# One layer of a hybrid attention trunk: attention's small products gathered into fewer bursts between the large products

## The chip, the cores and the metric

The kernel runs on one NeuronCore of a Trainium2 chip. The metric is the device time of one execution in microseconds (us); lower is better. TensorE (PE) does the matrix products, VectorE (DVE) and ScalarE (ACT) the elementwise work, SyncE (SP) issues the loads.

## The reference

One layer of a causal decoder trunk on 256 tokens of width 1024, in float32. One input projection of the normed input feeds two attentions side by side: eight heads of softmax attention (called MoBA in the code; the whole sequence is one block, so it is plain causal attention) and four heads of gated linear attention (GLA). Their outputs go through one output projection, and a gated feed-forward part of width 2816 follows.

```python
xn = rms_norm(x, attn_norm_g[l])
proj = xn @ w_in[l]
mq = rope(split_heads(proj[..., o_mq:o_mk], MOBA_HEADS), pos)
mk = rope(split_heads(proj[..., o_mk:o_mv], MOBA_HEADS), pos)
mv = split_heads(proj[..., o_mv:o_gq], MOBA_HEADS)
y_moba = merge_heads(moba_attention(mq, mk, mv))
...
og = gla_attention(gq, gk, gv, split_heads(log_a, GLA_HEADS))
...
x = x + jnp.concatenate([y_moba, y_gla], axis=-1) @ w_out[l]
hn = rms_norm(x, ffn_norm_g[l])
h = causal_dwconv(hn @ w_ffn_up[l], conv_w[l], conv_b[l])
h_gate, h_val = h[..., :D_FF], h[..., D_FF:]
x = x + (jax.nn.silu(h_gate) * h_val) @ w_ffn_down[l]
return rms_norm(x, final_norm_g)
```

## The kernel before, in words

The projections are the **large products**. Each float32 weight is split into a high and a low part (`split_hi`, line 92, ScalarE; `split_lo`, line 95, VectorE), and three products (`mm3`, lines 109 to 111) make one float32-exact sum. The input projection runs over q = 0 to 47: six groups of columns (G, q, k, v, gv, r) times eight contraction tiles. The output projection runs over q = 48 to 63, and behind it the feed-forward part runs over 22 pairs of column tiles to the end.

Attention is laid between the large products. A table `plan` says at which q a piece of attention is emitted: `on(q, f, ...)` appends it, and `emit(q)` calls what stands at q, in the order of the `on` calls, ahead of the large products of that q. On TensorE the instructions stand in just that order. On VectorE and ScalarE a scheduler of the language orders what was emitted.

The pieces that matter here are these.

- GLA's score matrix is built in seven levels (`LEVELS`, numbered 0 to 6 here). `lvl_a` and `lvl_b` (lines 329 to 331, 344, 350) make a level's factors on VectorE and ScalarE, in two pairs of tiles kt and qt that the levels use in turn. `lvl_c` is the level's product on TensorE (line 362; line 357 for level 6). `lvl_d_` is the level's copy out of its bank: a predicated copy on VectorE (line 376), or for level 6 a copy on ScalarE (line 371).
- Softmax attention goes by pairs of heads. `m_scores` (line 486) makes the scores of a pair in two banks. `m_softmax1` (lines 494, 496, 499) and `m_softmax2` (lines 505 to 507) make the probabilities of a head. `m_pt` transposes them, three transposes a head (line 514), with a copy on ScalarE (line 516). `m_av` is the value product of a pair (lines 526, 527), with its copies at lines 530 and 531.
- `l128_c` (line 401) and `g_av` (lines 418 to 421) are GLA's last products.

All these small products write to tiles that `att()` hands out from the pool `ps_att`: four PSUM banks, used in turn. A new tile waits until the last reader of its bank's tile before it is done. The transposes have a tile each, so has a level, a head's scores and a pair's value product.

The three transposes of a head are called pt0 to pt7 below, the value products av0 to av3, the level products c0 to c6, the scores s0 to s3. A **burst** is what stands on TensorE between two large products. The 16 bursts from q = 25 on are, before: c0; c1; c2 s0; c3 s1; pt0; pt1; c4 s2; pt2; c5 av0 pt3; s3; pt4; c6 av1 pt5; pt6; l128_c av2 pt7; g_av; av3.

Of the kernel before, what the change touches and what calls it, by code (L numbers as in the profile page):

```python
# [9 lines left out]
F32 = mybir.dt.float32  # L10
# [6 lines left out]
S = 256  # L17
KT = 8
HM, HD = 8, 64
# [6 lines left out]
EPS = 1e-6  # L26
NG = 256 + RANK + 256
LEVELS = [32, 16, 8, 4, 2, 1, 64]
# columns of the parameter array
P_FG, P_BG, P_CW, P_CB = 0, 8, 10, 10 + 3 * 2 * NP  # L30
# [4 lines left out]
def trunk_kernel(ctx: ExitStack, tc: tile.TileContext, xT_d, wG_d, w5_d, wo_d, up_d, dn_d,  # L35
# [16 lines left out]

    # ------------------------------------------------------------------ constants and parameters
    A.preload_act_table_set("natural_log_exp_and_others")
# [12 lines left out]

    # the tensor engine's clock rises while the first loads are under way
    warm = const.tile([128, 128], F32, name="warm")
# [4 lines left out]

    # ------------------------------------------------------------------ weights: load and split
    RAW, SPL = 4, 3
# [59 lines left out]

    # ------------------------------------------------------------------ x
    xg = main.tile([128, KT + KT * S], F32, name="xg")     # the first norm's gains, then x^T
    pag = xg[:, :KT]
# [33 lines left out]
    def rsqrt_t(r, ss, n, tmp):  # L173
        """r = (ss / n + EPS) ** -0.5 by logarithm and exponential, then a Newton step."""
        v, t = tmp
        V.tensor_scalar(v, ss, 1.0 / n, EPS, op0=ALU.mult, op1=ALU.add)
        A.activation(t, ss, AF.Ln, scale=1.0 / n, bias=eps)
        A.activation(r, t, AF.Exp, scale=-0.5)
        V.tensor_mul(t, r, r)
        V.scalar_tensor_tensor(t, t, -0.5, v, op0=ALU.mult, op1=ALU.mult)  # L180
        V.scalar_tensor_tensor(r, t, 1.5, r, op0=ALU.add, op1=ALU.mult)

    def rsqrt(r, ss, n, tmp):
        """r = (ss / n + EPS) ** -0.5: a seed from the exponent bits, then Newton steps. It yields
        between its steps, so that other work fits in."""
        v, t = tmp
        V.tensor_scalar(v, ss, 1.0 / n, EPS, op0=ALU.mult, op1=ALU.add)
        V.tensor_scalar(t.bitcast(I32), v.bitcast(I32), 1, None, op0=ALU.logical_shift_right)
        yield
        V.tensor_scalar(r.bitcast(I32), t.bitcast(I32), -1.0, float(0x5F3759DF),  # L190
                        op0=ALU.mult, op1=ALU.add)
        for _ in range(3):
            V.tensor_mul(t, r, r)
            yield
            V.scalar_tensor_tensor(t, t, -0.5, v, op0=ALU.mult, op1=ALU.mult)
            V.scalar_tensor_tensor(r, t, 1.5, r, op0=ALU.add, op1=ALU.mult)

    # ------------------------------------------------------------------ attention buffers
    ap_ = ctx.enter_context(ExitStack())
# [4 lines left out]
    Gc = at.tile([128, 512], F32, name="Gc")  # L204
    ATd = at.tile([128, 8, 64], F32, name="ATd")           # the blocks of 64 on the diagonal
    ATu = at.tile([128, 8, 64], F32, name="ATu")           # the second half's columns
    AT01 = at.tile([128, 4, 128], F32, name="AT01")
# [43 lines left out]
    def xrow():  # L251
        """The rotation's tables take up the norm, which lies along their rows here."""
        p = att()
        for tt in range(2):
            T.matmul(p[:, tt * 128:(tt + 1) * 128], rstd(tt).to_broadcast([128, 128]), ident,
                     start=True, stop=True)
        for t in (cos, sin):
            V.tensor_mul(t, t, p[:, :S])

    # ---- GLA  # L260
    def g_evac(tt):
# [19 lines left out]
    def g_diag():  # L281
        dgp = at.tile([128, 2, 256], F32, name="e", bufs=2)
        V.scalar_tensor_tensor(dgp, gqk[:, :, 0:256], DK ** -0.5, gqk[:, :, 272:528],
                               op0=ALU.mult, op1=ALU.mult)
        V.tensor_add(id64, ident[:, 0:64], ident[:, 64:128])
        dg = at.tile([128, 2, 2, 2], F32, name="dg")       # pair, ttile, head
        for tt in range(2):
            V.tensor_reduce(dg[:, :, tt, :], dgp[:, tt].rearrange("p (a h d) -> p a h d", a=2, h=2),
                            axis=mybir.AxisListType.X, op=ALU.add)
        for i in range(8):  # L290
            A.activation(ATd[:, i], id64, AF.Copy, scale=dg.rearrange("p a b c -> p (a b c)")[:, i:i + 1])
# [147 lines left out]
    def g_tail():  # L439
        # the norm's tables before the gate's: one change of tables  # L440
        with tc.manual_schedule(engines={mybir.EngineType.Activation}):
            for tt in range(2):
                g_norm(tt)
            for tt in range(2):
                gr_evac(tt)
# [12 lines left out]

    # ---- MoBA (the sequence is one block, so a query's own block is all it attends to)
    def rope_a(which, n):  # L460
        """The halves of each head change places."""
        qs = at.tile([128, 512], F32, name="qs", bufs=2)
        for i in range(4):
            a, b = 32 * i, 32 * (i ^ 1)
            A.activation(qs[a:a + 32], st["qk"[which]][n][b:b + 32], AF.Copy)  # L465
        st["rope", which, n] = qs.rearrange("p (a t) -> p a t", a=2)
# [12 lines left out]
    def m_scores(pr):  # L479
        # two heads in turn, each in its half of the array's rows and in a bank of its own  # L480
        for hh in range(2):
            st["s", 2 * pr + hh] = att()
        for c0, c1 in ((0, 128), (128, 384)):
            for hh in range(2):
                ps = slice(64 * hh, 64 * hh + 64)
                T.matmul(st["s", 2 * pr + hh][:, c0:c1], mqT[ps, pr, c0:c0 + 128], mkT[ps, pr, 0:c1 - c0],
                         start=True, stop=True)
# [44 lines left out]

    # ------------------------------------------------------------------ emission plan
    plan = {}

    def on(q, f, *a):
        plan.setdefault(q, []).append((f, a))
# [25 lines left out]
    for l in range(7):  # L563
        b = 21 + 11 * l // 4
        on(b, lvl_a, l)
        on(b + 1, lvl_b, l)
        on(b + 4, lvl_c, l)
        on(b + 5, lvl_d_, l)
    on(b + 5, lvl_join)
# [3 lines left out]
    for tt in range(2):  # L573
# [3 lines left out]
        on(40, gv_evac, tt)  # L577
    for h in range(HM):
        b = 30 + 3 * h // 2
        if h % 2 == 0:  # L580
            on(b, m_scores, h // 2)
        on(b + 1, m_softmax1, h)
        on(b + 2, m_softmax2, h)
        on(b + 4, m_pt, h)
        if h % 2:
            on(b + 7, m_av, h // 2)
    on(46, g_av, 0)
# [24 lines left out]
    for q in range(48):  # L612
        g, k = divmod(q, 8)
# [28 lines left out]

    # ------------------------------------------------------------------ output projection
    hh_ = main.tile([128, KT, S], F32R, name="hh", tag="ah")
# [33 lines left out]

    # ------------------------------------------------------------------ feed-forward
    downs = {}  # L680
# [91 lines left out]

    # the output's columns by bank; the last ones, which end the kernel, are fewer
    PIECES = (((0, 512), (512, 1024)), ((0, 512), (512, 768), (768, 1024)))
# [10 lines left out]
    def residual(tt, n):  # L785
        """The residual opens the down projection's sums."""
        a, b = PIECES[tt][n]
# [22 lines left out]

    # pair 0: its last contraction tile waits for the last columns of h
    up_alloc(0)
# [11 lines left out]
    lo(2, 1)  # L824
    # pair 1
    dload(1)
# [7 lines left out]
    for n, _ in enumerate(steps):  # L834
        if n < 4:
            ups[3].split_lo(512 * n, 512 * n + 512)
    # pair 2
    dload(2)
# [17 lines left out]
    gate_lo(0)  # L856
    # pair 3
    dload(3)
# [63 lines left out]
    A.preload_act_table_set("sqrt_and_others")  # L922
    # the last pair's gate is awaited behind one product of the second token tile
    for i in range(NP - 4, NP - 1):
# [10 lines left out]

    # ------------------------------------------------------------------ final norm
    fin = ff.tile([128, 24], F32, name="fin")
    yy = ff.tile([128, 2, D], F32, name="yy", tag="big")
    for tt in range(2):
# [4 lines left out]
        for n, (a, b) in enumerate(PIECES[tt]):  # L944
# [11 lines left out]
            if n < last:  # L956
                vb = v
                V.tensor_scalar(vh, v, -0.5, None, op0=ALU.mult)
        # r = (mean square + EPS) ** -0.5 with one Newton step
        A.activation(sq, ss, AF.Sqrt, scale=1.0 / D, bias=vb)  # L960
# [10 lines left out]
def _layout(inputs):  # L971
# [5 lines left out]
    def ktile(m):  # L977
        return m.reshape(-1, 128, m.shape[1]).transpose(1, 0, 2)      # [128, k, cols]

# [14 lines left out]
    fin_g = f(np.broadcast_to(a["final_norm_g"].reshape(1, D), (128, D)))  # L994
    # tables that depend on shapes alone
    inv = (1.0 / (np.float32(10000.0) ** (np.arange(0, HD, 2, dtype=np.float32) / np.float32(HD)))).astype(np.float32)
# [32 lines left out]
```

## Time and profile before

| | us |
|---|---|
| median of 3 runs (321.97 to 322.44) | 322.04 |
| span of the profiled execution, first to last instruction | 320.4 |
| what lies around the span (the difference of the two) | 1.6 |
| PE busy in the span | 312.3 |
| DVE busy in the span | 253.7 |
| ACT busy in the span | 203.2 |

The page gives the profiled execution by its span. With the 1.6 us around it, it stands for the median, 322.04 us. A busy PE is not a PE at its peak: matmuls are pipelined, so the distance from one start to the next tells what a product costs, and the duration of one does not. The rows in use are in the section after next.

### The profile page before, as it was taken

To read this page: it belongs to the slowest core of one execution; us is meant where nothing else is said; L and a number is where in the kernel's file an instruction comes from. 1 tells how busy PE (TensorE), PEld (TensorE's weight loads), DVE (VectorE), ACT (ScalarE), POOL (GpSimd) and SP (SyncE) were. 2 spreads that over 40 slices of the span, in tenths; PEclk is the share of its full clock that TensorE was granted. 3 is DMA by queue.
4 is the path that set the end of the run, shared out by engine and by line. 5 is a ranking of instruction groups with operands and counts; after the bars stand their busy time and mean duration, and the time that the engine had idled before them with its cause. 6 is when DMAs were issued, how large, how long until landed. Compare 5 with 4: busy or idle time off the path is not lost.

```text
span 320.4 us, 5873 instructions
## 1 busy us (share of the span) xinstructions
PE 312.3 (97%) x2312; PEld 285.9 (89%) x2312; DVE 253.7 (79%) x478; ACT 203.2 (63%) x369; POOL 3.5 (1%) x16
## 2 busy tenths in 40 slices
PE   8999999999999999999999999999999999999992
PEld 7999997776766999999999999999999999999982
DVE  3888999999634658899999987777787777776653
ACT  5978988588845748637677655555555555544353
POOL 4000000000000000000000000000000000000000
PEclk9999999999999999999999999999999999999997
DMA  6999433452360245379356555555555521110003
GB/s 186 387 415 402 183 133 131 139 186 79 125 262 1 103 163 190 140 282 370 127 212 254 202 196 196 199 196 198 197 196 199 218 111 68 65 67 1 2 0 132
DMA packets 12299, 55.39 MB, mean 173 GB/s; under 512 B 1376, under 2 KB 2928, under 8 KB 7920
## 3 DMA queue, kind: packets, MB, share of 16 engines
q1 hardware_dynamic: 12272, 55.02, 46.2%
q8 instruction: 18, 0.29, 0.4%
q14 instruction: 9, 0.07, 0.1%
HBM read 53.97 MB, written 1.05 MB: 172 GB/s over the span
## 4 chain that ended last, share of the span: by engine, by line
PE 79%; DVE 9%; ACT 5%; issue 2%; DMA 2%; SPq 1%; DVEq 0%; ACTq 0%
PE att L110 14%; PE att L109 14%; PE att L111 14%; PE acc L110 10%; PE acc L109 10%; PE acc L111 10%; DVE lo L95 2%; DMA xg<-in_xT 2%; ACT qs L465 1%; DVE qt L350 1%; DVE att L494 1%; PE att L421 1%; PE att L420 1%; PE att L526 1%; DVE ATd L376 1%
## 5 line engine op out<-in xcount | busy, mean ns | idle before, releaser
L92 ACT ACTIVATE hi<-raw 128x1024 fp32r<-128x1024 f32 (+3 forms) x84 | 80.1, 971 | 51.4 <-PE att L110 43.1
L95 DVE TENSOR_TENSOR lo<-raw,hi 128x1024 fp32r<-128x1024 f32 (+3 forms) x86 | 93.7, 1098 | 13.8 <-ACT hi L92 13.8
L109 PE MATMUL att<-hh,hi 128*128 128x256 f32 x352 | 98.6, 280 | 0.0
L111 PE MATMUL att<-hh,lo 128*128 128x256 f32 x352 | 98.4, 280 | 0.0
L110 PE MATMUL att<-hl,hi 128*128 128x256 f32 x352 | 98.4, 279 | 0.0
L109 PEld LDWEIGHTS att<-hh,hi 128*128 128x128 f32 x352 | 66.3, 188 | 0.0
L111 PEld LDWEIGHTS att<-hh,lo 128*128 128x128 f32 x352 | 66.2, 188 | 0.0
L110 PEld LDWEIGHTS att<-hl,hi 128*128 128x128 f32 x352 | 66.2, 188 | 0.0
L756 DVE SCALAR_TENSOR_TENSOR c<-us,par,c 128x256 f32<-128x256 f32 x88 | 40.7, 482 | 4.1 <-ACT c L748 2.5
L748 ACT ACTIVATE c<-us,par 128x256 f32<-128x256 f32 x44 | 24.0, 590 | 21.6 <-DVE us L738 16.1
L111 PE MATMUL acc<-dhi,gl 128*128 128x512 f32 (+1 forms) x88 | 32.3, 367 | 0.0
L110 PE MATMUL acc<-dlo,gh 128*128 128x512 f32 (+1 forms) x88 | 32.2, 366 | 0.0
L109 PE MATMUL acc<-dhi,gh 128*128 128x512 f32 (+1 forms) x88 | 31.8, 361 | 0.0
L695 DVE TENSOR_TENSOR dlo<-draw,dhi 128x1024 fp32r<-128x1024 f32 x22 | 26.7, 1220 | 0.0
L738 DVE TENSOR_TENSOR us<-att,rb 128x512 f32<-128x512 f32 x20 | 13.8, 690 | 15.9 <-PE att L111 15.9
L109 PE MATMUL acc<-hi,ah 128*128 128x512 f32 (+1 forms) x64 | 25.9, 404 | 0.2 <-ACT hi L92 0.2
L110 PE MATMUL acc<-lo,ah 128*128 128x512 f32 (+1 forms) x64 | 24.6, 384 | 0.4 <-DVE lo L95 0.4
L111 PE MATMUL acc<-hi,al 128*128 128x512 f32 (+1 forms) x64 | 24.1, 376 | 0.0
L690 ACT ACTIVATE dhi<-draw 128x1024 fp32r<-128x1024 f32 x22 | 23.1, 1048 | 0.0
L110 PEld LDWEIGHTS acc<-dlo,gh 128*128 128x128 f32 x88 | 16.5, 188 | 3.0
L109 PEld LDWEIGHTS acc<-dhi,gh 128*128 128x128 f32 x88 | 16.6, 188 | 2.9
L111 PEld LDWEIGHTS acc<-dhi,gl 128*128 128x128 f32 x88 | 16.5, 188 | 2.6
(192 smaller groups left out, 537.5 us busy)
## 6 DMA issues: line engine op xcount, KB each, us to landing
raw<-in_up SPq DMA_DIRECT2D x22, 1024.0 KB, 4.8
draw<-in_dn SPq DMA_DIRECT2D x22, 512.0 KB, 5.7
raw<-in_w SPq DMA_DIRECT2D x8, 1024.0 KB, 7.4
raw<-in_wo SPq DMA_DIRECT2D x4, 1024.0 KB, 4.7
raw<-in_w SPq DMA_DIRECT2D x4, 512.0 KB, 7.6
raw<-in_wG SPq DMA_DIRECT2D x2, 528.0 KB, 7.2
out_y<-yy SPq DMA_DIRECT2D x4, 256.0 KB, 2.2
raw<-in_wG SPq DMA_DIRECT2D x3, 264.0 KB, 4.8
```

The source lines that it names most:

```text
L92: A.activation(self.hi[:, a:b], self.raw[:, a:b], AF.Copy)
L95: V.tensor_sub(self.lo[:, a:b], self.raw[:, a:b], self.hi[:, a:b])
L109: T.matmul(out, sh, mh, start=first, stop=False, **kw)
L110: T.matmul(out, sh, ml, start=False, stop=False, **kw)
L111: T.matmul(out, sl, mh, start=False, stop=last, **kw)
L350: V.tensor_mul(o, q_, e_)
L376: V.copy_predicated(o, m, p[:, :256].rearrange("p (i n b) -> p i n b", i=8, b=b))
L690: A.activation(hi, downs[i][0], AF.Copy)
L695: V.tensor_sub(lo, d, hi)
L738: V.tensor_tensor(u[:, :, 2:], upo[i][2].rearrange("p (a t) -> p a t", a=2), rb[:, None, :].to_broadcast([128, 2, S]), op=ALU.mult)
L748: A.activation(cv[i][:, a], u[:, a, 2:], AF.Identity, bias=par[:, P_CB + m:P_CB + m + 1], scale=par[:, P_CW + 2 * 2 * NP + m:P_CW + 2 * 2 ...
L756: V.scalar_tensor_tensor(c[:, a], u[:, a, w:w + S], par[:, wc:wc + 1], c[:, a], op0=ALU.mult, op1=ALU.add)
```

## The change

Three places of the plan change. Level 0's product moves from q = 25 to q = 27 and its copy from 26 to 28, so c0 and c1 stand in one burst. The transposes of the two heads of a pair are emitted together, at q = 35, 38, 41 and 44, behind the value product of the pair before, which stands at the same q. The last value product, av3, moves from q = 47 to q = 46, ahead of `g_av`. The ten bursts are then: c0 c1; c2 s0; c3 s1; pt0 pt1; c4 s2; c5 av0 pt2 pt3; s3; c6 av1 pt4 pt5; l128_c av2 pt6 pt7; av3 g_av. No instruction is added or removed.

```diff
     for l in range(7):
         b = 21 + 11 * l // 4
         on(b, lvl_a, l)
         on(b + 1, lvl_b, l)
-        on(b + 4, lvl_c, l)
-        on(b + 5, lvl_d_, l)
+        on(b + 4 if l else 27, lvl_c, l)
+        on(b + 5 if l else 28, lvl_d_, l)
...
-    for h in range(HM):
-        b = 30 + 3 * h // 2
-        if h % 2 == 0:
-            on(b, m_scores, h // 2)
-        on(b + 1, m_softmax1, h)
-        on(b + 2, m_softmax2, h)
-        on(b + 4, m_pt, h)
-        if h % 2:
-            on(b + 7, m_av, h // 2)
+    for pr in range(HM // 2):
+        b = 30 + 3 * pr
+        on(b, m_scores, pr)
+        for hh in range(2):
+            on(b + 1 + hh, m_softmax1, 2 * pr + hh)
+            on(b + 2 + hh, m_softmax2, 2 * pr + hh)
+        on(min(b + 8, 46), m_av, pr)
+        on(b + 5, m_pt, 2 * pr)
+        on(b + 5, m_pt, 2 * pr + 1)
```

The rest of the diff drops comments. Lines from 640 on stand two further down.

The first place is TensorE at q = 38, before (c5, av0, pt3). Numbers are those of buffers: att_960 is c5's bank tile, att_972 that of av0, att_979 that of pt3; the name in brackets is the engine whose count the instruction waits for.

```order
L362 MATMUL att_960<-qt1_131,kt1_129 64x64 [waits DVE_49]
L362 MATMUL att_960<-qt1_131,kt1_129 64x64 x7
L526 MATMUL att_972<-pt_863,mv_143 64x256 [waits Activation_49]
L527 MATMUL att_972<-pt_863,mv_143 64x128
L526 MATMUL att_972<-pt_885,mv_143 64x256
L527 MATMUL att_972<-pt_885,mv_143 64x128
L514 MATMUL att_979<-ident_78,pe_894 128x128 [waits Activation_49]
L514 MATMUL att_979<-ident_78,pe_894 128x128 x2
```

The same place now (c5 is att_954, av0 att_966, pt2 att_973, pt3 att_979):

```order
L362 MATMUL att_954<-qt1_131,kt1_129 64x64 [waits DVE_49,Activation_49]
L362 MATMUL att_954<-qt1_131,kt1_129 64x64 x7
L526 MATMUL att_966<-pt_879,mv_143 64x256 [waits DVE_49,PE_49]
L527 MATMUL att_966<-pt_879,mv_143 64x128
L526 MATMUL att_966<-pt_885,mv_143 64x256
L527 MATMUL att_966<-pt_885,mv_143 64x128
L514 MATMUL att_973<-ident_78,pe_863 128x128 [waits Activation_49]
L514 MATMUL att_973<-ident_78,pe_863 128x128 x2
L514 MATMUL att_979<-ident_78,pe_894 128x128 [waits DVE_49]
L514 MATMUL att_979<-ident_78,pe_894 128x128 x2
```

pt2 has come into this burst, six large products later than it was, and pt3 now waits for VectorE where it waited for ScalarE. In the built program pt3's tile lies in the bank that c5 used in the same burst, so the count it waits for is that of c5's copy (line 376). Before, its bank was that of pt2, which ScalarE had copied out.

The second place is VectorE where it makes c5's copy, before (c5 is att_960; kt0 and qt0 are level 6's factors, d_1002 belongs to `l128_a`, pe_947 to head 4):

```order
L95 TENSOR_TENSOR lo_951<-raw_664,hi_950 128x1024 [waits DMAHW0_49,Activation_49]
L505 RECIPROCAL mx_943<-mx_943 128x2 [waits Activation_49]
L385 TENSOR_TENSOR d_1002<-Gc_123 128x256
L507 TENSOR_SCALAR pe_947<-pe_947,mx_943 128x256 [waits DVE_49]
L376 COPY_PREDICATED ATd_124<-lvl_77,att_960 128x256 [waits PE_49]
L344 TENSOR_TENSOR kt0_128<-gkT_122,e_933 128x4x64 [waits Activation_49]
L350 TENSOR_TENSOR qt0_130<-gqT_121,e_933 64x4x64 x2
L531 TENSOR_TENSOR ml_98<-att_972,mh_326 128x256 [waits Activation_49]
```

And now (c5 is att_954):

```order
L95 TENSOR_TENSOR lo_945<-raw_664,hi_944 128x1024 [waits DMAHW0_49,Activation_49]
L344 TENSOR_TENSOR kt0_128<-gkT_122,e_933 128x4x64 [waits Activation_49]
L350 TENSOR_TENSOR qt0_130<-gqT_121,e_933 64x4x64 x2
L505 RECIPROCAL mx_937<-mx_937 128x2
L376 COPY_PREDICATED ATd_124<-lvl_77,att_954 128x256 [waits DVE_49,PE_49]
L531 TENSOR_TENSOR ml_98<-att_966,mh_326 128x256 [waits Activation_49]
L507 TENSOR_SCALAR pe_941<-pe_941,mx_937 128x256 [waits DVE_49]
L385 TENSOR_TENSOR d_1002<-Gc_123 128x256
```

Level 6's three factor products have moved ahead of c5's copy, and one `l128_a` difference and one scaling of probabilities have moved behind it.

The third place is TensorE at q = 46, as a piece of the difference (gv, ATd and ATu are GLA's values and scores):

```order
+L526 MATMUL att<-pt,mv 64x256
+L527 MATMUL att<-pt,mv 64x128
+L526 MATMUL att<-pt,mv 64x256
+L527 MATMUL att<-pt,mv 64x128
 L420 MATMUL att<-gv,ATd 64x128
 L421 MATMUL att<-gv,ATu 64x128
```

av3 now stands right ahead of `g_av`; it stood alone between the large products of q = 46 and those of q = 47.

## Rows read from the trace of the kernel before

**Rows 1.** The page: granted TensorE clock in 40 slices of the span, in tenths

```profile
PEclk9999999999999999999999999999999999999997
```

**Rows 2.** The page: chain that ended last, by engine

```profile
PE 79%; DVE 9%; ACT 5%; issue 2%; DMA 2%; SPq 1%; DVEq 0%; ACTq 0%
```

**Rows 3.** Waits of PE: waiter, releaser, us in total, times, longest

```profile
PE att L526 <- ACT pe L499: 0.6, 1, 0.6
```

**Rows 4.** Timeline of PE around c0 (columns: start us, us, engine line op)

```profile
46.27 0.40 PE L110 MATMUL acc<-lo,ah 128*128 128x512 f32 x1
46.50 0.40 PE L111 MATMUL acc<-hi,al 128*128 128x512 f32 x1
46.83 0.69 PE L362 MATMUL att<-qt,kt 128*64 128x64 f32 x16
47.44 0.50 PE L109 MATMUL acc<-hi,ah 128*128 128x512 f32 x1
47.78 0.40 PE L110 MATMUL acc<-lo,ah 128*128 128x512 f32 x1
```

**Rows 5.** Timeline of PE around pt2

```profile
70.63 0.40 PE L111 MATMUL acc<-hi,al 128*128 128x512 f32 x1
70.86 0.49 PE L514 MATMUL att<-ident,pe 128*128 128x128 f32 x3
71.11 0.48 PE L109 MATMUL acc<-hi,ah 128*128 128x512 f32 x1
71.43 0.39 PE L110 MATMUL acc<-lo,ah 128*128 128x512 f32 x1
```

**Rows 6.** Timeline of PE, av0 and pt3 in the burst behind c5

```profile
73.94 0.66 PE L526 MATMUL att<-pt,mv 128*64 128x256 f32 x4 [0.57 <-ACT pe L499]
...
74.75 0.55 PE L514 MATMUL att<-ident,pe 128*128 128x128 f32 x3
75.05 0.48 PE L109 MATMUL acc<-hi,ah 128*128 128x512 f32 x1
```

**Rows 7.** Timeline of DVE around c5's copy

```profile
74.80 0.41 DVE L385 TENSOR_TENSOR d<-Gc 128x256 f32<-128x256 f32 x1
75.12 0.35 DVE L507 TENSOR_SCALAR pe<-pe,mx 128x256 f32<-128x256 f32 x1
75.38 0.73 DVE L376 COPY_PREDICATED ATd<-lvl,att 128x256 f32<-128x256 int32 x1
75.90 0.46 DVE L344 TENSOR_TENSOR kt<-gkT,e 128x256 f32<-128x256 f32 x1
76.28 0.84 DVE L350 TENSOR_TENSOR qt<-gqT,e 64x256 f32<-64x256 f32 x2
```

**Rows 8.** Timeline of PE behind av3, the first two large products

```profile
102.31 0.50 PE L109 MATMUL acc<-hi,ah 128*128 128x512 f32 x1
102.65 0.39 PE L110 MATMUL acc<-lo,ah 128*128 128x512 f32 x1
```

**Rows 9.** Timeline of ACT around level 6's copy

```profile
82.92 1.07 ACT L92 ACTIVATE hi<-raw 128x1024 fp32r<-128x1024 f32 x1
83.87 0.51 ACT L516 ACTIVATE pt<-att 128x384 f32<-128x384 f32 x1
84.24 0.41 ACT L530 ACTIVATE mh<-att 128x256 fp32r<-128x256 f32 x1
84.51 0.60 ACT L371 ACTIVATE ATu<-att 64x512 f32<-64x512 f32 x1
```

**Rows 10.** Stretches at the end: busy us per engine, granted clock, DMA

```profile
314.64:316.77 2.13, 0.00 (x0) 0.00 (x0) 1.78 (x9) 1.25 (x4) 0.00 (x0) 1.00 0.15 55
316.77:320.40 3.63, 0.00 (x0) 0.00 (x0) 0.01 (x1) 0.24 (x1) 0.00 (x0) 0.50 0.37 144
```

**Rows 11.** Timeline of PE in the first large products

```profile
4.22 0.59 PE L109 MATMUL acc<-hi,ah 128*128 128x272 f32 x1 [0.24 <-ACT hi L92]
...
9.69 0.28 PE L109 MATMUL att<-hi,ah 128*128 128x256 f32 x1
```

## The prediction

> **What bounds the kernel now.** I read the page first. PE is busy from end to end, and its granted clock is full in all slices but the last [rows 1], so no clock is to be won here. The chain that ended last is PE's for 79% of the span [rows 2]. PE's list of waits holds one wait inside the attention stretch: 0.6 us of a value product (line 526), ended by ScalarE's exponentials [rows 3]. So an instruction slot taken off TensorE behind that wait is worth its full time, and one taken off ahead of it is worth nothing unless the wait goes too.
>
> The timeline of PE then prices a burst. Large products of 512 columns start 0.23 us apart (46.27 to 46.50) [rows 4]. In front of c0 the distance is 0.33, and behind it the first large product takes 0.34 until the next start [rows 4]. So a burst of small products costs 0.10 us going in and 0.11 coming out, besides its own products. For a burst of transposes the entry costs nothing (70.63 to 70.86 is 0.23), the three transposes take 0.25, and the exit 0.32 - 0.23 = 0.09 [rows 5].
>
> **The change part by part.**
>
> Fewer bursts. c0 and c1 joined save one entry and one exit, 0.21 us. pt0 with pt1, pt2 with av0, pt4 with av1, and pt6 with av2 each save one exit of a transpose burst, 4 x 0.09 = 0.36. Of these, pt0 with pt1 and pt2 with av0 stand ahead of or in the burst of c5, the other two behind it. av3 joined to `g_av` saves an entry, taken as c0's 0.10, and an exit of 0.34 - 0.23 = 0.11 [rows 4, 8]; I take 0.20. All together 0.77 us. That is the whole gain in view, and it is little: 0.64 us is 0.2% of 322.04, about what a measurement of this kernel can tell from no change.
>
> The old wait. In the burst c5 av0 pt3 the value product waited 0.57 us for the exponentials of the next pair's first head [rows 6], because they were the last reader of its bank. In the new order av0 waits for VectorE instead, for the copy of c4; that copy is one of the instructions ahead of c5's on VectorE. pt2, behind av0, takes the bank of those exponentials.
>
> The new wait. pt3 now takes the bank that c5 filled earlier in the same burst, and it waits for c5's copy on VectorE (line 376). When does that copy end? Before, it started at 75.38 and took 0.73, so it ended at 76.11 [rows 7]. Nobody on PE needed it so early. In the new order level 6's factors stand ahead of it: line 344 takes 75.90 to 76.28, 0.38 us, and line 350 twice takes 0.84, together 1.22. What has gone behind it is line 385 (74.80 to 75.12, 0.32) and one scaling (75.12 to 75.38, 0.26) [rows 7], together 0.58. VectorE has no pause here, its instructions follow each other, so the copy ends at 76.11 + 1.22 - 0.58 = 76.75. Two short waits of VectorE on ScalarE ahead of it may shrink in the new order; I take 76.6 and keep 76.4 and 76.9 as ends.
>
> PE would reach pt3 long before. It was at av0 by 73.37 (73.94 less the 0.57 of idling) [rows 6]. The savings ahead of it are 0.21 + 0.09, and pt2's own burst of 0.25 + 0.09 is gone from there [rows 5], so now it is there at 72.7. av0 takes 0.81 (73.94 to 74.75) [rows 6] and pt2 0.25. PE is at pt3 by 73.8, or some tenths later if av0 waits a little for c4's copy, and then stands for 2.5 to 2.8 us. All that was saved ahead of here, and the old 0.57, are swallowed by this wait.
>
> pt3 starts at 76.65 and takes 0.30 (74.75 to 75.05) [rows 6], so the next large product starts at 76.95. In the kernel before it started at 75.05, with the same products behind it. That is **1.90 us later**; with the ends 1.7 to 2.2.
>
> Behind it. pt4 and pt6 give back 0.18, av3 0.20. A second bank can bite: pt5 now waits for ScalarE's copy of level 6 (line 371). PE gets to it at about 82.82 (the 0.30 of pt4 behind 82.52, where pt5 stood) + 1.6 = 84.4. The copy ended at 84.51 + 0.60 = 85.11, of which the two copies ahead of it, 83.87 to 84.51, stand behind it in the new order: 84.47 [rows 9]. I charge 0.1 for it; its ends are 0 and the 1.07 of a split that stands ahead of it on ScalarE [rows 9].
>
> The rest of the span is dense on PE: no other wait of attention's kind stands in the list [rows 3], so a delay at 77 us is still there at the end. SP's loads, POOL's work and the number of instructions are unchanged, and the loads run ahead of their use; a shift of under 2 us on the splits is passed on to them and back, at no cost.
>
> Sum: + 1.90 - 0.38 + 0.10 = + 1.62 us. Against the profiled execution, 320.4 of span and 1.6 around it, which equals the median of the three runs: 322.0 + 1.6 = **323.6 us**.
>
> **A rule against the change.** The rows show a bank that is wanted again before VectorE has emptied it. The Trainium skill, Perfetto Trace Analysis, section Optimizing Tensor Performance, asks that independent groups of products rotate through different PSUM banks so that the copy out of one overlaps the next group's products. The pool here has four banks; two are held by the next pair's scores, and the new burst asks for four tiles. By that rule the burst stalls, and the sum above says by how much.
>
> **The rivals.**
>
> *The clock falls in the pause.* At the end of the span PE stands idle from 314.64, at full clock until 316.77, 2.13 us later, and from there at 0.50, the 1.2 GHz level [rows 10]. A pause of 2.5 us at 74 us is no shorter. Against it: there the engine had nothing to do any more, here products come back. The price: at the start PE had large products from 4.22 on, and only at 9.69 do they start 0.12 us apart and not 0.22 [rows 11]. If it takes as long again, half of 5.5 us is lost, 2.7; if the clock is back in half that time, 1.35. That gives 325.0 to 326.3, most likely the lower end. Chance 0.25.
>
> *The second bank costs more.* If the split of 1.07 us [rows 9] stands between level 6's product and its copy in full, pt5 waits up to 1 us more: 324.0 to 324.7. Chance 0.10.
>
> *The pool holds, and the kernel gets faster.* If c5's copy ends by 74.0, when PE comes to pt3, nothing waits there, and both the 0.77 of the bursts and the 0.57 of the old wait are won: 322.04 - 1.34 = 320.7. The place is line 376 on VectorE; the price is the 1.34. Against it speaks that the copy ended at 76.11 even in the order that favoured it [rows 7]. The Trainium skill, Perfetto Trace Analysis, section Matmul Optimizations, holds that products should execute back to back in batches, which is this change's direction. The trace agrees with it to the 0.21 us of a burst's two ends, no further. Chance 0.05.
>
> *No change.* If the copy ended at about 75.0 to 75.4, the wait would cost what the bursts give back: 321.5 to 322.6. It needs VectorE to be 1.4 us faster over ten instructions. Chance 0.10. That the change doesn't do what it says I leave out: the order shows ten bursts in place of 16.
>
> **How the numbers follow.** The forecast, 323.0 to 324.0 around 323.6, has 0.50; the four rivals have 0.25, 0.10, 0.05 and 0.10. The range 322.7 to 326.0 takes in the forecast, the second bank and most of the clock's case; it leaves out the faster case, nearly all of no change and the upper end of the clock. Slower by over 0.2%, above 322.7: 0.50 + 0.25 + 0.10 = 0.85. Within 0.2%: 0.10. Faster: 0.05.
>
> **What would show it.** In the profile after, PE's list of waits should have a wait of line 514 on VectorE's line 376 of about 2.6 us between 73 and 77 us, and the wait of line 526 on line 499 gone or short. The first large product behind pt3 should start near 76.9. The distances of 0.33 and 0.34 around c0 should appear once for c0 and c1. The granted clock should read full through 80 us; a stretch at half there, with large products about twice as far apart as now, is the first rival. If line 514 waits for nothing and the span falls below 320, the bank argument is wrong.

## The result, and the profile after

| | before | after |
|---|---|---|
| median, us | 322.01 (321.97 to 322.44, 4 runs) | 325.33 (324.35 to 325.62, 4 runs) |
| ratio, 95% interval | 1 | 1.0096 (1.008 to 1.0111) |
| profiled execution, us | 322.0 | 325.62 |
| its span, us | 320.4 | 323.8 |
| mean granted clock | 0.994 | 0.993 |

The changed kernel is slower by 3.3 us. The forecast was 323.6, and the time lies in the range, near its upper end. Two things were lost, not one: the wait for a bank, as forecast, and on top of it the clock, which was the first rival and not the forecast.

The page of the kernel after, clock row (it answers to [rows 1]):

```profile
PEclk9999999997999999999999999999999999999999
```

A 7 stands in the tenth slice, at 73 to 81 us. PE's waits, where before there was only the 0.6 of line 526 [rows 3] (waiter, releaser, us in total, times, longest):

```profile
PE att L514 <- DVE ATd L376: 1.9, 1, 1.9
...
PE att L526 <- DVE ATd L376: 0.4, 1, 0.4
...
PE att L514 <- DVE pe L507: 0.2, 1, 0.2
```

The first is pt3's wait for c5's copy. The old wait is gone, and two short ones have come: av0's for c4's copy, and pt1's for a scaling of probabilities. The timeline of PE around the burst of c5 (start us, us, engine line op, idle before and releaser), answering to [rows 6]:

```profile
72.26 0.69 PE L362 MATMUL att<-qt,kt 128*64 128x64 f32 x16
73.33 0.66 PE L526 MATMUL att<-pt,mv 128*64 128x256 f32 x4 [0.38 <-DVE ATd L376]
...
74.14 0.55 PE L514 MATMUL att<-ident,pe 128*128 128x128 f32 x3
76.56 0.84 PE L514 MATMUL att<-ident,pe 128*128 128x128 f32 x3 [1.88 <-DVE ATd L376]
77.05 0.78 PE L109 MATMUL acc<-hi,ah 128*128 128x512 f32 x1
77.63 0.63 PE L110 MATMUL acc<-lo,ah 128*128 128x512 f32 x1
78.05 0.63 PE L111 MATMUL acc<-hi,al 128*128 128x512 f32 x1
...
79.89 1.00 PE L486 MATMUL att<-mkT,mqT 64*128 64x128 f32 x8
80.83 0.50 PE L109 MATMUL acc<-hi,ah 128*128 128x512 f32 x1
81.17 0.40 PE L110 MATMUL acc<-lo,ah 128*128 128x512 f32 x1
```

pt2 ends the work that PE has, and it stands for 1.88 us. pt3 comes at 76.56. Then the large products are 0.42 us apart (77.63 to 78.05), not 0.23 as in [rows 4], and after the scores at 79.89 the pace is back. The timeline of VectorE shows why pt3 waits that long, answering to [rows 7]:

```profile
74.50 0.44 DVE L344 TENSOR_TENSOR kt<-gkT,e 128x256 f32<-128x256 f32 x1
74.83 0.88 DVE L350 TENSOR_TENSOR qt<-gqT,e 64x256 f32<-64x256 f32 x2
75.72 0.17 DVE L505 RECIPROCAL mx<-mx 128x2 f32<-128x2 f32 x1
75.81 0.70 DVE L376 COPY_PREDICATED ATd<-lvl,att 128x256 f32<-128x256 int32 x1
```

Level 6's factors (lines 344 and 350) stand ahead of the copy, which starts at 75.81.

pt3 falls on c5's bank although it is only the third tile behind c5 in a pool of four. The description of the kernel says that the banks are used in turn; that is not strictly so, for a bank that is still held is passed over. In the built program c5, av0, pt2 and pt3 share three banks, and the fourth holds the scores of head 5, which ScalarE still reads when pt3 has started (timeline of ScalarE):

```profile
76.66 0.36 ACT L499 ACTIVATE pe<-att,mx 128x128 f32<-128x128 f32 x1
```

The slow large products have a row in the view by stretches (us, busy us per engine, granted clock, DMA):

```profile
74.60:76.55 1.95, 0.08 (x1) 0.00 (x0) 1.92 (x7) 0.68 (x3) 0.00 (x0) 1.00 0.01 4
76.68:80.09 3.41, 3.41 (x11) 2.37 (x13) 2.92 (x8) 2.71 (x9) 0.00 (x0) 0.50 0.17 19
80.10:85.00 4.90, 4.90 (x31) 3.73 (x33) 2.50 (x13) 3.17 (x8) 0.00 (x0) 1.00 0.48 201
```

In the pause PE does nothing and the clock is still full. From 76.68 to 80.09, that is 3.41 us, it is granted half, the 1.2 GHz level, though PE is busy all the time. Then it is full again.

To compare profiles without the start, whose length differs between profiles (the first large product of v starts at 44.71 to 46.66), I take one stretch from each: from the first large product of v (45.34 before, 45.22 after) to the last product of the kernel (314.36 before, 317.52 after). It is 269.02 us before and 272.30 after, 3.28 more. The column "stretch" of this table is the difference from 269.02.

| kernel | median, us | before, same chip | ratio, 95% interval | stretch, us |
|---|---|---|---|---|
| eight products in the pause | 324.11 | 322.01 | 1.0057 (1.0045 to 1.007) | +1.85 |
| pair 1's join alone | 324.74 | 322.01 | 1.0085 (1.006 to 1.011) | +3.57 |
| pair 1's join alone, again | 324.62 | 322.09 | 1.0088 (1.0059 to 1.0118) | +2.03 |
| changed kernel, again | 324.47 | 322.11 | 1.0084 (1.0056 to 1.0111) | +3.28 |
| changed kernel, third time | 324.12 | 322.09 | 1.0067 (1.0039 to 1.0095) | +3.29 |
| c5's copy earlier | 323.08 | 321.94 | 1.0037 (1.0022 to 1.0051) | +1.01 |
| pt2 back | 322.59 | 321.94 | 1.0019 (1.001 to 1.0029) | +0.53 |
| c0 with c1, av3 with `g_av`, alone | 322.00 | 321.94 | 1.0005 (0.9996 to 1.0014) | -0.18 |
| transposes in other banks | 322.03 | 322.01 | 0.9996 (0.9987 to 1.0005) | -0.09 |
| and pair 3's scores later | 321.71 | 322.01 | 0.9988 (0.9979 to 0.9996) | -0.33 |
| and pt0 apart | 321.10 | 321.94 | 0.9977 (0.9968 to 0.9986) | -0.89 |
| and pt1 later | 320.91 | 322.11 | 0.9966 (0.9953 to 0.9978) | -1.15 |

### The profile page after: what moved, and what is told of

Same layout as the page of the kernel before. It is cut to its first block, busy times and chain, and to the rows that moved or that the text cites. A ratio compares the mean times of both kernels' runs of the same rounds, so it can differ in the third digit from the quotient of the medians.

```text
span 323.8 us, 5874 instructions
## 1 busy us (share of the span) xinstructions
PE 313.4 (97%) x2312; PEld 286.7 (89%) x2312; DVE 254.1 (78%) x478; ACT 203.8 (63%) x369; POOL 3.5 (1%) x16
## 4 chain that ended last, share of the span: by engine, by line
PE 84%; DVE 7%; ACT 3%; DMA 2%; SPq 1%; issue 1%; ACTq 0%; DVEq 0%
PE att L111 14%; PE att L109 14%; PE att L110 14%; PE acc L110 12%; PE acc L109 12%; PE acc L111 12%; DVE lo L95 2%; DMA xg<-in_xT 2%; ACT qs L465 1%; DVE qt L350 1%; DVE att L494 1%; PE att L421 1%; PE att L420 1%; PE att L514 1%; DVE ATd L376 1%
```

## The experiments

### Is the second loss the clock, and is the pause its cause?

The changed kernel with eight large products put into the pause:

```diff
+    def fill(n):
+        h_, l_ = slots[4 + 2 * 3 + 1].view(512)
+        for _ in range(n):
+            T.matmul(st["v"][0], ah[:, 6, 0:128], h_[:, 2], start=True, stop=True)
...
         on(b + 5, m_pt, 2 * pr)
+        if pr == 1:
+            on(b + 5, fill, 8)
         on(b + 5, m_pt, 2 * pr + 1)
```

> The changed kernel plus eight more large products between pt2 and pt3, into a bank of v that has been copied out; their results are not used. Nothing else moves: c5's copy (line 376) ends at 76.5 as before. Theory (the loss is the wait for that copy, about 1.6 us, and on top of it the granted clock's fall in the pause, about 1.7 us): eight products of 0.23 us take 1.84 us and fill the pause of 1.88 us, so they cost almost nothing of their own, the wait of line 514 shrinks from 1.88 to below 0.3 us, the granted clock reads full through 80 us, and the time is 323.4 to 324.0. Rival 1 (the half clock at 76.7 has another cause than the pause, for instance the small products around it): the clock falls all the same and the time stays at 325.0 to 325.7. Rival 2 (the copy on VectorE is held up by PE and moves too): the pause stays and the eight products come on top, 327.

The timeline of PE, same place (line 522 is the filling):

```profile
74.01 2.11 PE L522 MATMUL acc<-hi,ah 128*128 128x512 f32 x8
76.16 0.55 PE L514 MATMUL att<-ident,pe 128*128 128x128 f32 x3
76.47 0.48 PE L109 MATMUL acc<-hi,ah 128*128 128x512 f32 x1
...
78.03 0.93 PE L486 MATMUL att<-mkT,mqT 64*128 64x128 f32 x8
78.89 0.50 PE L109 MATMUL acc<-hi,ah 128*128 128x512 f32 x1
```

And the view by stretches:

```profile
76.68:80.09 3.41, 3.41 (x20) 2.36 (x19) 3.31 (x10) 2.49 (x8) 0.00 (x0) 1.00 0.22 38
```

pt3 has no wait left, the clock is full, and the eight extra products make the kernel 1.2 us faster than 325.33, at 324.11 (0.1 above the interval that was expected). So the clock falls because of the pause, not because of the small products around it, which are all still there. The price comes out of the same work in two profiles: from pt3's start to the first large product behind the scores it is 76.56 to 80.83 in the changed kernel, 4.27 us, and 76.16 to 78.89 here, 2.73 us. The half clock cost 1.54 us.

The Trainium skill, TensorE: Matmul & The Clock Gate, section "A second HAM failure mode: psum-queue depth-cycling", tells of a kernel that often idles briefly between groups as it cycles through PSUM banks and pays for a clock that swings between its levels. The trace agrees in part: here it is not many idles but one, of 1.88 us for a bank, with 1.54 us paid behind it.

### Is it this one join?

The kernel before with pt2 alone moved behind av0:

```diff
-        on(b + 4, m_pt, h)
+        on(38 if h == 2 else b + 4, m_pt, h)
```

> The kernel before with one edit: pt2 goes behind av0 into pt3's burst, all else as it was. Theory (this one join carries the whole loss): c4's and c5's copies stand as in the changed kernel, pt3 waits for line 376 until about 76.5, +1.9 us against before, the clock falls in the pause as in the changed kernel, +1.7, and none of the small gains of the other joins (0.4) is there: 325.2 to 326.0, as slow as the changed kernel or slower by some tenths. Rival (the loss is spread over all the joins, or the half clock comes from other bursts): 322.2 to 324.0.

The profiled run shows both losses (timeline of PE, and the view by stretches):

```profile
76.41 0.55 PE L514 MATMUL att<-ident,pe 128*128 128x128 f32 x3 [2.27 <-DVE ATd L376]
...
76.95:80.30 3.35, 3.35 (x13) 2.31 (x13) 2.37 (x6) 2.29 (x7) 0.00 (x0) 0.50 0.24 56
```

The stretch is +3.57, more than the whole change. One join carries the loss. The median, 324.74, is below what was expected, though: of six runs three lie at 323.79 to 324.16 and three at 325.33 to 326.56.

### Does the clock fall in every run?

One of the first four runs of the changed kernel lay 1 us below the others as well. Here is the same kernel again, as it is:

> The changed kernel as it is, in more runs and with a profile of its own. Open is whether the clock falls in the pause in every run: six runs of the kernel with pair 1's join alone lie at 323.8 to 324.2 and at 325.3 to 326.6, and one of four of the changed kernel lies 1 us below the others. Theory (the pause is at the edge, and the fall comes in some runs only): the runs lie in two groups about 1.5 us apart, at 323.6 to 324.3 and 325.1 to 325.7. Rival (the fall comes in every run, and the lower ones are scatter): all within 0.6 us around 325.3.

Three of six runs lie at 323.80 to 323.94, two at 325.0 and 325.07. The profiled one, 327.1, has the fall and a late start too: its large product of v comes at 46.66, 1.32 us after that of the kernel before, while its stretch, +3.28, is that of the first profile. Its pt3 and the stretch behind it:

```profile
78.00 0.62 PE L514 MATMUL att<-ident,pe 128*128 128x128 f32 x3 [1.86 <-DVE ATd L376]
...
78.36:81.74 3.38, 3.38 (x14) 2.35 (x14) 2.59 (x7) 2.47 (x8) 0.00 (x0) 0.50 0.26 39
```

A third profile of the changed kernel, and a second one of pair 1's join alone:

> The changed kernel as it is, for one more profile. Ten runs of it so far lie at 323.8 to 324.4 (four), at 325.0 to 325.6 (five) and at 327.1; the two profiles are of the upper ones, and both show the clock's fall. Theory (the lower runs are those without the fall): if the profiled run lies at 323.6 to 324.4, its clock is full through 85 us, with the wait of 1.9 us in place; if it lies above 325.0, the clock falls right behind pt3's start. Rival (the two groups come from something else): a low run with a fall, or a high one without it and without a late start.

The profiled run is an upper one, 325.18, and shows the fall (stretch +3.29):

```profile
76.06 0.73 PE L514 MATMUL att<-ident,pe 128*128 128x128 f32 x3 [1.87 <-DVE ATd L376]
...
76.30:79.69 3.39, 3.39 (x13) 2.35 (x13) 2.77 (x7) 2.59 (x8) 0.00 (x0) 0.50 0.23 34
```

The five runs lie at 323.61, 323.77, 324.12, 325.18 and 325.51.

> The kernel with pair 1's join alone, for one more profile; six runs of it lie at 323.8 to 324.2 (three) and 325.3 to 326.6 (three). Theory: a profiled run below 324.5 has a full clock through 85 us and the wait of 2.3 us, one above 325.0 has the fall. Rival: a low run with a fall, or a high one without it and without a late start.

This profile is of a low run, 323.76. Its timeline of PE:

```profile
76.23 0.55 PE L514 MATMUL att<-ident,pe 128*128 128x128 f32 x3 [2.26 <-DVE ATd L376]
76.53 0.48 PE L109 MATMUL acc<-hi,ah 128*128 128x512 f32 x1
...
78.10 0.93 PE L486 MATMUL att<-mkT,mqT 64*128 64x128 f32 x8
78.96 0.50 PE L109 MATMUL acc<-hi,ah 128*128 128x512 f32 x1
```

And its stretch:

```profile
76.68:80.09 3.41, 3.41 (x20) 2.36 (x20) 3.41 (x14) 2.50 (x9) 0.00 (x0) 1.00 0.25 38
```

The wait is whole, 2.26 us, and the clock stays full. The stretch is +2.03, against +3.57 in the profile with the fall: 1.54 us again. So the two groups of runs are runs with and without the fall. Of 15 runs of the changed kernel seven lie at 323.61 to 324.35 and eight at 325.0 or above. No low run of the changed kernel itself has a profile, but every run has a mean granted clock, and it divides them in the same way: 0.989 to 0.993 in the eight, 0.997 or 0.998 in six of the seven. The seventh, 324.35, has 0.994, the value of the kernel before in its profile, where the half clock lies at the end alone [rows 10]. The ten runs of pair 1's join alone divide likewise: 0.989 to 0.993 in the five upper ones, 0.997 to 0.999 in the five lower ones. Without the fall the median of the changed kernel is 323.89.

### Is the wait set by the copy's place on VectorE?

The changed kernel with c5's copy emitted one step earlier:

```diff
-        on(b + 5 if l else 28, lvl_d_, l)
+        on((28 if l == 0 else b + 4 if l == 5 else b + 5), lvl_d_, l)
```

> The changed kernel with one edit: c5's copy (line 376) is emitted one step earlier, right behind its product, so that it stands ahead of level 6's factors on VectorE. Theory (the wait of pt3 is set by the place of that copy on VectorE, and the fall of the clock by the length of the pause): the copy ends some 1.0 us earlier, line 514 waits 0.8 to 1.0 us in place of 1.88, the granted clock stays full through 80 us, and both parts of the loss shrink: 322.6 to 323.3, without the spread of the runs whose clock falls. Rival (the clock falls at any pause at this place): the wait shrinks by 1 us, but the clock falls all the same, 324.0 to 324.6.

The wait is 0.95 us, half of what it was:

```profile
75.13 0.55 PE L514 MATMUL att<-ident,pe 128*128 128x128 f32 x3 [0.95 <-DVE ATd L376]
```

The copy now starts at 74.37, behind line 344 but ahead of line 350. The granted clock is full behind the wait:

```profile
75.20:80.00 4.80, 4.80 (x26) 3.58 (x27) 4.75 (x20) 4.45 (x13) 0.00 (x0) 1.00 0.26 56
```

The five runs lie at 322.85 to 323.34, without two groups, and their mean granted clocks are 0.996 to 0.999. Both parts of the theory hold.

### What is left if pt2 goes back?

```diff
-        on(b + 5, m_pt, 2 * pr)
+        on(b + 5 - (pr == 1), m_pt, 2 * pr)
```

> The changed kernel with one edit: pt2 goes back to the burst of its own behind c4's, as in the kernel before; the other joins stay. Theory: pt3 takes the bank that it had and waits for nothing, the clock stays full, and the loss of 3.3 us goes. With PE on time again the join of pt4 with pt5 shows its own bank wait: pt5 waits for ScalarE's copy of level 6 (line 371), which the late PE of the changed kernel never met, up to 1.3 us. The time is 322.4 to 323.2, still no faster than the kernel before. Rival (the join of pair 1 is the only one that costs): no wait of line 514 over 0.3 us, 321.6 to 322.0.

The waits of PE:

```profile
PE att L362 <- DVE mx L496: 0.7, 1, 0.7
PE att L514 <- ACT ATu L371: 0.5, 1, 0.5
...
PE att L514 <- DVE pe L507: 0.2, 1, 0.2
```

The big loss is gone, and the second bank now shows: pt5 waits 0.5 us for level 6's copy on ScalarE (line 371). A third wait, 0.7 us, has come at c5 itself, behind a head's softmax on VectorE (line 496). The joined order meets one wait or another, and the kernel is still 0.2% slower than before.

### What do the other parts give alone?

The kernel before with c0 joined to c1 and av3 to `g_av`:

```diff
-        on(b + 4, lvl_c, l)
-        on(b + 5, lvl_d_, l)
+        on(b + 4 if l else 27, lvl_c, l)
+        on(b + 5 if l else 28, lvl_d_, l)
...
-            on(b + 7, m_av, h // 2)
+            on(min(b + 7, 46), m_av, h // 2)
```

> The kernel before with two parts of the change alone: c0 with c1, and av3 with the last value products. No transposes move. The traces so far show the first at -0.35 us and the second at -0.18. Theory: the first stands ahead of av0's wait for the exponentials (0.57 us), which grows by as much, so only a part of it is kept: 321.6 to 321.9. Rival (the wait of av0 is for something that comes earlier too when PE comes earlier): both are kept, 321.4 to 321.6.

322.00, no difference that the interval (0.9996 to 1.0014) can tell, and less than I expected. The stretch says -0.18, and that is av3. c0 with c1 gains 0.35 us where it stands, but it is lost before av0 is reached: a wait for VectorE's scaling (line 507) has come in the middle of pt1, at 66.12 us (0.2 us by the list of waits). pt1 takes 0.66 us until the next large product (65.65 to 66.31) where it took 0.29 (66.02 to 66.31), and av0 starts at 73.95 with 0.57 of idling, as in [rows 6] to 0.01 us.

### Other banks

The changed kernel with all transposes in banks of v and gv that have been copied out:

```diff
-            p = att()
+            p = st["v" if h < 4 else "gv"][h % 2]
```

> The changed kernel with one edit: the transposes of all eight heads go to two banks of the other pool, those of v (heads 0 to 3) and of gv (heads 4 to 7), which have been copied out by then and are not opened again until later. Theory (the wait of pt3 is for a bank, not for its data): line 514 waits no more for line 376, the granted clock stays full, and the joined bursts keep their gains; the next tile of the old pool that falls on c5's bank is a score of pair 3 (line 486), which may wait up to 0.7 us for the same copy. The time is 321.3 to 322.0. Rival (VectorE and ScalarE are late themselves, and PE only meets them at the bank): the wait of 1.9 us turns up whole at the next product, and the time stays at 323.5 or more.

Line 514 no longer waits for line 376, and the clock is full: 322.03, 0.03 above the interval expected. The wait was for a bank, not for data. But it is no faster than the kernel before. The score products of pair 3, of which one tile gets c5's bank, take 1.16 us here where they took 0.93 before, and the joins of transposes turn out to give nothing (below). Next, pair 3's scores one step later:

```diff
-        on(b, m_scores, pr)
+        on(b + (pr == 3), m_scores, pr)
```

> As the last one, and pair 3's scores one step of the order later (40 in place of 39), so that they too come to c5's bank after its copy. Theory: no wait of PE over 0.4 us is left between 68 and 95 us, the old 0.57 of av0 is mostly won and so are the exits of the joined bursts; the time is 321.0 to 321.5, faster than the kernel before by 0.5 to 1.0 us. Rival (pair 3's softmax is then late for pt6): the wait comes back at line 514 near 92 us and the time is that of the last kernel or longer, 321.5 to 322.5.

321.71: the scores take 0.93 again, but the wait of 0.38 for c4's copy is left at av0, and the time is 0.2 us above the interval expected. Then pt0 apart again (the loop of the kernel before, with these places):

```diff
-            on(b, m_scores, h // 2)
+            on((30, 33, 36, 40)[h // 2], m_scores, h // 2)
...
-        on(b + 4, m_pt, h)
         if h % 2:
-            on(b + 7, m_av, h // 2)
+            on((38, 41, 44, 46)[h // 2], m_av, h // 2)
+        on((34, 35, 38, 38, 41, 41, 44, 44)[h], m_pt, h)
```

> As e_best1 (transposes in the banks of v and gv, pair 3's scores one step later), with pt0 back in the burst of its own. The traces so far show that pt0 with pt1 costs: PE loses 0.36 us against the kernel before between 59.8 and 69.4 us, of which 0.18 is a wait of pt1 for VectorE's scaling (line 507), and the joined transposes of two heads take 0.63 us where two bursts took 0.25 and 0.30 and one exit of 0.09. Theory: pt0 apart gives back 0.2 to 0.35: 321.2 to 321.6. Rival (the loss there belongs to pt1's wait in either order): 321.6 to 321.8, as e_best1.

321.10, 0.1 below the interval expected, and for another reason than expected. The wait for line 507 stays at 0.20 us; what has gone is the 0.38 of av0 behind c5. The loss between 59.8 and 69.4 us belongs to pt1 in either order, as the rival said, though its time was not met either. So pt1 one step later, 36 in place of 35:

> As e_best2, with pt1 one step later, so that VectorE's scaling (line 507) is done when PE comes to it. Theory (the 0.36 us that every variant with c0 and c1 joined loses between 59.8 and 69.4 us is pt1's wait for that scaling, data and not a bank): the wait of line 507 goes from PE's list, and 0.2 to 0.45 us are won: 320.6 to 320.9. Rival (the loss is VectorE's pace there, and the next product waits for it): 321.0 to 321.2, as e_best2.

Behind the start nothing is left of PE's waits; from 20 to 312 us it is busy all the time (view by stretches):

```profile
20.00:312.00 292.00, 292.00 (x2191) 267.73 (x2191) 237.24 (x441) 186.65 (x339) 0.22 (x3) 1.00 0.45 164
```

The timeline of PE around c5 (one line is added, so line 515 is the transposes and 527 the value product):

```profile
71.74 0.69 PE L362 MATMUL att<-qt,kt 128*64 128x64 f32 x16
72.25 0.65 PE L527 MATMUL att<-pt,mv 128*64 128x256 f32 x4
...
73.05 0.87 PE L515 MATMUL acc<-ident,pe 128*128 128x128 f32 x6
```

av0 follows c5 with no idling, and so do pt2 and pt3. The time is 320.91 against 322.11, a gain of 0.34% (interval 0.22 to 0.47). It beats both kernels. The stretch gains 0.26 us on the last one, of the 0.36 that were in question.

## Why the prediction was right, and where it was wrong

**The new wait: right.** The step said that pt3 waits for line 376 and starts at 76.65. It started at 76.56, or 76.68 when both profiles are laid over each other at the first product of v (45.22 and 45.34). With the 0.30 that pt3 takes at full clock the next large product would start at 76.98, against 75.05 in [rows 6]: +1.93, where 1.90 was forecast. The copy ended at 76.51 (75.81 + 0.70), or 76.63 when laid over, where 76.6 was taken. The wait itself is 1.88 and not 2.6: the end was right and not the start. c5 started 0.30 earlier than before (72.26, laid over 72.38, against 72.68) and not 0.64 (the 0.30 saved and the 0.34 of pt2's own burst), because pt1's wait had taken the rest. Then av0 waited 0.38 for c4's copy, which the step had allowed for with "some tenths".

**The exits of transpose bursts: wrong.** The step took 0.09 for each, from the exit of pt2's burst [rows 5]. pt4 and pt5 in one burst (timeline of PE after):

```profile
85.54 0.87 PE L514 MATMUL att<-ident,pe 128*128 128x128 f32 x6
86.17 0.48 PE L109 MATMUL acc<-hi,ah 128*128 128x512 f32 x1
```

Six transposes take 0.63. Apart they took 0.25 and 0.30, with one exit of 0.09 more: 0.64. Three more transposes make a burst 0.33 longer (0.63 less 0.30), while alone they take 0.25 and an exit of 0.09, 0.34. So pt4 and pt6 gave 0.02 together, not 0.18.

**av3: right,** 0.18 (forecast 0.20). **c0 with c1: mis-sized.** The joined burst:

```profile
49.51 1.15 PE L362 MATMUL att<-qt,kt 128*64 128x64 f32 x32
50.59 0.50 PE L109 MATMUL acc<-hi,ah 128*128 128x512 f32 x1
50.93 0.40 PE L110 MATMUL acc<-lo,ah 128*128 128x512 f32 x1
```

Its products take 1.08 us (49.51 to 50.59), where c0 alone took 0.61 [rows 4], so twice that is 1.22: the gain is 0.21 and 0.14 more. That it is swallowed was right; that the wait behind c5 swallows it was not, pt1's wait for line 507 does.

**The second bank: not met in the changed kernel.** The 0.10 for pt5 was not paid there, because PE comes so late. In the kernel with the pause filled, where the clock stays full, the burst of pt4 and pt5 takes 0.72 (83.61 to 84.33) and not 0.63, and level 6's copy ends in the middle of it, at 83.97 (83.39 + 0.58). That fits a wait of 0.09, but no list of waits names it. With pt2 back the wait is 0.5, inside the bounds of 0 and 1.07.

**The clock: the step that failed.** The sum held no loss of clock. "The forecast, 323.0 to 324.0 around 323.6, has 0.50", and the fall 0.25. The price given, 1.35 to 2.7 with the lower end likelier, fits the 1.54 measured. The weight did not: "there the engine had nothing to do any more, here products come back" was taken as a reason against, but in all four profiles with the fall the products had come back before it, and it came all the same. By their times and their granted clocks, eight of 15 runs had the fall. The sum without it, 1.93 - 0.02 - 0.18 = 1.73, plus 1.54 is 3.27, and the stretch shows 3.28. In the runs without the fall the median, 323.89, lies 0.3 above the forecast.

**Luck.** 325.33 lies outside the 323.0 to 324.0 of the forecast, and the wider range held it only because it took in the clock's case. Which case a median shows is chance as well: three of the first four runs are of the upper group, and five later runs of the same kernel have the median 324.12. Within the sum, two errors worked against each other: the exits of pt4 and pt6 gave 0.16 less than was counted, and the second bank took 0.10 less. So 1.73 lies nearer to the forecast's 1.62 than its terms do.

## What to carry to other kernels

Before small products are gathered into one burst, count the banks that the burst asks for and those that are still held, and look where the copy that frees the last of them stands on its engine; if there are fewer free banks than tiles, the burst waits for that copy, whatever else it saves. A pause of TensorE like this one, of about 2 us inside a dense stretch, is to be priced twice, by its length and by a stretch at half clock behind it, and the forecast then has two times, not one. Price a join from the whole burst and not from its edges, and look for free banks in another pool, which here turned a loss of 3.3 us into a gain of 1.2.

## What the runs showed of the hardware

The granted clock fell to half behind pauses of 1.86, 1.87 and 1.88 us (three profiles of the changed kernel) and of 2.27 us (pair 1's join alone). In another profile of that last kernel it stayed full behind 2.26 us. So with pauses of 1.9 to 2.3 us at this place the same kernel has runs with the fall and runs without. With the pause of 0.95 us (c5's copy earlier) the profile shows none. What decides it in a run stays open: no run here was made to set it.

In none of the four did the fall come in the pause itself. It came when pt3 had already started, 0.1 to 0.5 us before (76.56 and 76.68 in the first), and the half clock then lay on large products that kept PE busy throughout.
